# Reading the decode's gate sums from a small SBUF tile that ScalarE fills, in place of PSUM

## The chip, the core and the metric

The kernel runs on one core of a Trainium2 chip. TensorE (PE in the profile, with PEld for its weight loads) multiplies matrices into PSUM; VectorE (DVE) and ScalarE (ACT) do the elementwise work and read PSUM; GpSimd (POOL) does small elementwise work and issues gathers; SyncE (SP) issues most of the other transfers. Each engine takes its own instructions in the order in which the program lists them. The metric is the device time of one execution in microseconds (us), lower is better; the median of several executions stands for a kernel.

## What is computed

One layer of a decoder for two groups of rows that share the weights: a prompt of 1024 rows and eight sample rows, each of these with a paged cache of 8192 earlier positions. The part that the change touches is the attention of the eight sample rows. Every cached position and head carries a forget logit; a score is the query times the key plus a sum of these logits from behind that position up to the end:

```python
lf_all = jnp.concatenate([logf_pool[page_table].reshape(B, past, H).astype(jnp.float32), logf], axis=1)
c = jnp.cumsum(lf_all, axis=1)
...
s = jnp.einsum('bqhd,bkhd->bhqk', q, k).astype(jnp.float32) * (ATT_HEAD_DIM ** -0.5)
s = s + (cq.astype(jnp.float32).transpose(0, 2, 1)[:, :, :, None]
         - ck.astype(jnp.float32).transpose(0, 2, 1)[:, :, None, :])
p = jax.nn.softmax(s, axis=-1).astype(v.dtype)
return jnp.einsum('bhqk,bkhd->bqhd', p, v)
```

## The kernel before

The prompt's work (`prompt`, large matrix products with fp32 values split into a high and a low part, three products each: lines 270 to 274) and the samples' work (`sample`, which is `decode` and then `sample_rest`) are written as two Python generators. The loop at line 1923 runs the prompt's generator and, by a table of paces (`PACE`, line 76), takes pieces of the samples' generator in between. That fixes the order in which instructions are written; the order in which each engine gets them is worked out when the program is built, by a scheduler that walks a simulated timeline (`schedule_with_timeline_sim=True`, line 2013) and takes on each engine what is ready there. Some blocks bind that order: `behind(e)` (line 1369) keeps an instruction behind a named earlier one of the same engine, and `tc.high_priority()` moves one up.

`decode` (line 1374) handles the samples one after the other, sixteen chunks of keys each. For sample b, `kstep` (line 1425) has GpSimd gather a chunk of keys into a `kv` buffer (line 1428), and VectorE multiplies them with the query and sums them into the scores `s` (lines 1435 and 1436 while the prompt is in its attention, lines 1444 and 1448 elsewhere). There are four `kv` buffers, which keys and values share; `vstep` (line 1487) gathers values (line 1489), and TensorE multiplies them with the exponentials (line 1495).

In chunk 11 of a sample, `gates_scan` gathers the sample's logits (line 1404); ScalarE reorders them from position-major to head-major into the tile `A` (line 1407), and VectorE makes running sums over the 64 positions of each partition and head (line 1408). In chunk 13, `gates` (line 1411) adds the last running sum of each head to a small term (`tot`, line 1413). TensorE multiplies `tot` with a constant matrix of ones and zeros (line 1418), which gives in PSUM, in a tile `ms`, the sum over all later partitions: 128 x 8 numbers. VectorE then subtracts `A`, read with a step of 64 elements, from those 8 numbers, each broadcast over 64 positions, into the tile `dec` (line 1420). `soft_max` (line 1457) adds `dec` to the scores in line 1460, after the sixteenth chunk.

The tile `ms` has one buffer, one bank of PSUM (`MS`, line 152). It is free for its next user only when the last reader is done. The other users are the samples' softmax (lines 1468 and 1481), the later samples' stage, and the prompt's attention in its first half: there every third of the small accumulators comes from `MS` and the others from `BB` (`B3`, line 825), for the transposes of line 836 and the products of line 852. ScalarE empties these with lines 843 and 861, or VectorE with line 841.

Weights for the prompt come from memory into `wr`; ScalarE rounds them into `wh` (line 235) and VectorE subtracts to get `wl` (line 236); five and four buffers of these stand between the two engines and TensorE.

Of the kernel before, what the change touches and what calls it, by code (L numbers as in the profile page):

```python
# [11 lines left out]
AF = mybir.ActivationFunctionType  # L12
ALU = mybir.AluOpType
# [5 lines left out]
P = 128  # L19
# [59 lines left out]
def build(nc, tc, ctx, a, phases=None):  # L79
# [27 lines left out]
    def nm(s):  # L107
        cnt[0] += 1
        return f"{s}_{cnt[0]}"
# [16 lines left out]
    def sm(shape, tag, bufs=2, dt=F32):  # L126
        return small.tile(shape, dt, tag=tag, bufs=bufs, name=nm(tag))
# [24 lines left out]
    def MS():  # L152
        return BB() if MB else psum.tile([P, 512], F32, tag="ms", bufs=1, name=nm("ms"))
# [1215 lines left out]
    def behind(e):  # L1369

        return tc.issue_after(last[e]) if e in last else nullcontext()


    def decode():
# [36 lines left out]
        def gates(b, A):  # L1411
            tot = sm([P, 8], "tot", 2)
            nc.vector.tensor_tensor(
                tot, A.rearrange("p (h k) -> p h k", k=64)[:, :, 63], lfz[:, b * 8 : b * 8 + 8], op=ALU.add
            )
            ps = MS()
            with behind(ENG.PE):
                mmul(ps[:, :8], suf, tot, start=True, stop=True)
            dt_ = dec("dec").rearrange("p (k h) -> p k h", h=8)
            nc.vector.tensor_tensor(  # L1420
                dt_, ps[:, :8].unsqueeze(1).broadcast_to((P, 64, 8)), A.rearrange("p (h k) -> p k h", k=64), op=ALU.subtract
            )
            return dt_

# [99 lines left out]
        st, A, dt_, pm, dg, dv, vm = ([None] * 8 for _ in range(7))  # L1524
        pend = []
        st[0] = prep(0)
        for g in range(8 * 16 + 16 + VLAG + 2):
# [8 lines left out]
            if b < 8:  # L1536
                left = yield from kstep(b, ch, st[b])
                if ch == 11:
                    A[b] = gates_scan(b)
                if ch == 13:  # L1540
                    dt_[b] = gates(b, A[b])
                if ch == 14 and b < 7:
                    st[b + 1] = prep(b + 1)
                if ch == 15:
                    pm[b] = soft_max(b, st[b], dt_[b])
# [489 lines left out]
```

## Time and profile before

| | |
|---|---|
| runs of the kernel before (us) | 1798.83, 1797.29, 1791.11; median 1797.29 |
| the profiled execution (us) | 1793.69, of which 1791.7 lie in the profile's span |
| granted TensorE clock in it | 0.993 of full speed |
| transfers | 521.06 MB, mean 291 GB/s |

A row of the profile that begins with a line number is a group of instructions: line, engine, operation, tiles written and read, shapes, count, then busy microseconds and the mean nanoseconds of one, then the engine's idle time just before them and who ended it. A row of the instructions of one line gives, after the count, the minimum, median and maximum duration in nanoseconds and the first and the last start. A row of the timeline begins with the start and the duration in microseconds; an "x" count behind it is the number of neighbouring instructions merged. A row of waits gives the total, the number and the longest. A row of the table by stages gives the stretch, its length, and the busy time of each engine with its number of instructions, then clock, DMA share and GB/s.

### The profile page before, as it was taken

The numbers are of one execution on the slowest core, as the hardware profiler recorded it, in microseconds if no ns is written. First come the engines' busy times: TensorE is split into PE (matmuls) and PEld (weight loads), VectorE is DVE, ScalarE is ACT, GpSimd is POOL, SyncE is SP. The second block draws the span as 40 slices with busy tenths as digits, with TensorE's granted clock in tenths as the row PEclk, the third lists the DMA queues.
The fourth block names the chain that finished last, engine by engine and source line by source line (L and its number), as shares of the span: only waits on it lengthen the run. The fifth ranks groups of instructions, "written<-read, shape, count | busy, mean of one in ns | idle before, by whom it ended". The sixth has DMA issues, their size and how long they took to land.

```text
span 1791.7 us, 25124 instructions
## 1 busy us (share of the span) xinstructions
PE 1735.9 (97%) x9653; PEld 1285.7 (72%) x9653; DVE 1399.9 (78%) x1733; ACT 733.5 (41%) x1374; POOL 488.3 (27%) x461
## 2 busy tenths in 40 slices
PE   8999999889999999999999999999999999999997
PEld 5787777655677666767777777766666778768875
DVE  4689658989788986989999999898885549855344
ACT  6332355566643635333333244335353233333232
POOL 1252234443222332333322223433322112102110
PEclk9999999999999999999999999999999999999999
DMA  8786798777697975779788788988879587568982
GB/s 291 297 304 226 294 334 319 259 264 244 254 403 279 363 299 224 282 285 345 290 301 313 291 317 311 376 306 346 320 280 350 214 306 249 191 260 297 359 310 80
DMA packets 157074, 521.06 MB, mean 291 GB/s; under 512 B 20874, under 2 KB 40842, under 8 KB 124186
## 3 DMA queue, kind: packets, MB, share of 16 engines
q0 software_dynamic: 57168, 341.14, 50.0%
q1 hardware_dynamic: 92874, 165.73, 26.5%
q10 hardware_dynamic: 6912, 12.59, 1.9%
q8 instruction: 76, 1.25, 0.3%
q14 instruction: 44, 0.36, 0.1%
HBM read 495.47 MB, written 23.93 MB: 290 GB/s over the span
## 4 chain that ended last, share of the span: by engine, by line
PE 53%; issue 9%; DMA 8%; DVE 6%; ACT 2%; POOL 2%; POOLq 0%; DVEq 0%; ACTq 0%; SPq 0%
DMA kv<-cache_v,io 6%; PE ba L272 6%; PE ba L274 6%; PE ba L273 6%; PE dv L1495 4%; PE bb L272 3%; PE bb L273 3%; PE bb L274 3%; PE ba L1063 1%; DVE s L1448 1%; PE ba L1064 1%; PE ba L1065 1%; PE dv L331 1%; DMA kv<-cache_k,io 1%; PE dv L1774 1%
## 5 line engine op out<-in xcount | busy, mean ns | idle before, releaser
L235 ACT ACTIVATE wh<-wr 128x1024 fp32r<-128x1024 f32 (+2 forms) x220 | 228.6, 1044 | 443.3 <-PE ba L273 142.3
L236 DVE TENSOR_TENSOR wl<-wr,wh 128x1024 fp32r<-128x1024 f32 (+2 forms) x220 | 262.7, 1200 | 165.1 <-PE ba L274 57.4
L1428 POOL DMA_INDIRECT kv<-cache_k,io x128 | 186.9, 1460 | 606.8 <-DVE s L1448 327.2
L1444 DVE TENSOR_TENSOR kv<-kv,d 128x1024 f32<-128x1024 f32 (+1 forms) x156 | 258.0, 1681 | 32.6 <-DMA kv<-cache_k,io 32.6
L1448 DVE TENSOR_REDUCE s<-kv 128x16 f32<-128x1024 f32 (+1 forms) x156 | 258.4, 1672 | 0.0
L1489 POOL DMA_INDIRECT kv<-cache_v,io x128 | 160.8, 1256 | 239.4 <-PE dv L1495 155.2
L272 PE MATMUL ba<-u,wh 128*128 128x512 f32 x528 | 209.3, 397 | 0.0
L274 PE MATMUL ba<-u,wl 128*128 128x512 f32 x528 | 209.0, 396 | 0.0
L273 PE MATMUL ba<-u,wh 128*128 128x512 f32 x528 | 208.5, 395 | 0.5 <-DVE u L239 0.5
L272 PE MATMUL ba<-wh,u 128*128 128x512 f32 (+1 forms) x495 | 186.1, 379 | 0.9 <-ACT u L235 0.9
L273 PE MATMUL ba<-wl,u 128*128 128x512 f32 (+1 forms) x495 | 185.1, 375 | 1.3 <-DVE wl L236 1.3
L274 PE MATMUL ba<-wh,u 128*128 128x512 f32 (+1 forms) x495 | 183.4, 375 | 0.0
L1495 PE MATMUL dv<-kv,s 128*32 128x512 f32 x1024 | 127.1, 598 | 1.6 <-DMA kv<-cache_v,io 1.6
L274 PEld LDWEIGHTS ba<-u,wl 128*128 128x128 f32 x528 | 99.2, 188 | 29.0 <-issue 6.5
L272 PEld LDWEIGHTS ba<-u,wh 128*128 128x128 f32 x528 | 99.3, 188 | 26.4 <-issue 4.8
L273 PEld LDWEIGHTS ba<-u,wh 128*128 128x128 f32 x528 | 99.2, 188 | 25.2 <-issue 2.3
L272 PEld LDWEIGHTS ba<-wh,u 128*128 128x128 f32 x495 | 93.0, 188 | 25.0 <-issue 6.5
L272 PE MATMUL bb<-u,wh 128*128 128x512 f32 x272 | 108.7, 400 | 0.0
L274 PE MATMUL bb<-u,wl 128*128 128x512 f32 x272 | 108.0, 398 | 0.0
L273 PE MATMUL bb<-u,wh 128*128 128x512 f32 x272 | 107.9, 397 | 0.0
L273 PEld LDWEIGHTS ba<-wl,u 128*128 128x128 f32 x495 | 93.0, 188 | 20.1 <-DVE wl L236 1.9
L274 PEld LDWEIGHTS ba<-wh,u 128*128 128x128 f32 x495 | 92.9, 188 | 19.5 <-issue 1.6
(454 smaller groups left out, 3310.6 us busy)
## 6 DMA issues: line engine op xcount, KB each, us to landing
wr<-w_up SPq DMA_DIRECT2D x88, 512.0 KB
kv<-w_up POOLq DMA_DIRECT2D x22, 1024.0 KB
wr<-w_down SPq DMA_DIRECT2D x40, 512.0 KB
kv<-w_down POOLq DMA_DIRECT2D x11, 1024.0 KB
wr<-w_in SPq DMA_DIRECT2D x16, 512.0 KB
wr<-w_o SPq DMA_DIRECT2D x16, 512.0 KB
wr<-w_cq SPq DMA_DIRECT2D x16, 512.0 KB
wr<-w_co SPq DMA_DIRECT2D x16, 512.0 KB
```

What stands on the lines that cost most here:

```text
L235: nc.scalar.activation(h, src, AF.Copy)
L236: nc.vector.tensor_tensor(l, src, h.bitcast(F32), op=ALU.subtract)
L272: mmul(out, sh, mh, start=(i == 0), stop=False)
L273: mmul(out, sh, ml, start=False, stop=False)
L274: mmul(out, sl, mh, start=False, stop=(i == n - 1))
L331: mmul(ps[32 * j : 32 * j + 32, :w], xT[:, k, :] if nk == 8 else xT[:, k * 8 : k * 8 + 32], raw[:, q, j * w : (j + 1) * w], start=(k == 0) ...
L1063: mmul(pss[i], mh[k][:, tb], wh, start=(k == korder[0]), stop=False)
L1428: nc.gpsimd.indirect_dma_start(kv, None, a["cache_k"], off(kidx[:, b, ch : ch + 1]))
L1444: nc.vector.tensor_tensor(kvv[:, i : i + m, :], kvv[:, i : i + m, :], qb.unsqueeze(1).broadcast_to((P, m, 512)), op=ALU.mult)
L1448: nc.vector.tensor_reduce(s[:, ch * 4 + i : ch * 4 + i + m, :].rearrange("p k h -> p (k h)"), kvv[:, i : i + m, :].rearrange("p k (h d) -> ...
L1489: nc.gpsimd.indirect_dma_start(kv, None, a["cache_v"], off(kidx[:, b, ch : ch + 1]))
L1495: mmul(dv[32 * j : 32 * j + 32, :], s[:, ch * 4 : ch * 4 + 4, :].rearrange("p k h -> p (k h)"), kvv[:, j, :], start=(ch == 1), stop=(ch == ...
```

## The change

```diff
             ps = MS()
             with behind(ENG.PE):
                 mmul(ps[:, :8], suf, tot, start=True, stop=True)
+            sfs = sm([P, 8], "sfs", 2)
+            nc.scalar.activation(sfs, ps[:, :8], AF.Copy)
             dt_ = dec("dec").rearrange("p (k h) -> p k h", h=8)
             nc.vector.tensor_tensor(
-                dt_, ps[:, :8].unsqueeze(1).broadcast_to((P, 64, 8)), A.rearrange("p (h k) -> p k h", k=64), op=ALU.subtract
+                dt_, sfs.unsqueeze(1).broadcast_to((P, 64, 8)), A.rearrange("p (h k) -> p k h", k=64), op=ALU.subtract
             )
```

`sfs` is an SBUF tile of 128 x 8 fp32 numbers with two buffers. ScalarE copies the eight columns of `ms` into it; VectorE's subtraction takes the broadcast operand from `sfs`. So `ms` has ScalarE's copy as its only reader, and the subtraction waits for ScalarE where it waited for TensorE. Each of the eight samples runs this once.

## The prediction

> **What bounds the kernel now.** I read the page's busy times first, then the table by stages, then what TensorE waited for.
>
> ```profile
> span 1791.7 us, 25124 instructions
> ...
> PE 1735.9 (97%) x9653; PEld 1285.7 (72%) x9653; DVE 1399.9 (78%) x1733; ACT 733.5 (41%) x1374; POOL 488.3 (27%) x461
> ```
>
> TensorE is idle for 1791.7 - 1735.9 = 55.8 us in all. An edit that leaves TensorE's own work as it is can win some of that and no more; it can lose without such a limit. The stages show where the idle time lies (columns: stretch, its length, then the busy time of each engine):
>
> ```profile
> core 0: us, PE busy (x) PEld busy (x) DVE busy (x) ACT busy (x) POOL busy (x), PEclk, DMA share, GB/s
> ...
> 270.00:505.00 235.00, 214.97 (x1378) 152.24 (x1377) 206.36 (x356) 141.07 (x309) 82.73 (x106) 0.97 0.78 276
> ...
> 700.00:1000.00 300.00, 298.49 (x1419) 223.30 (x1418) 279.84 (x261) 105.72 (x167) 86.35 (x63) 1.00 0.78 294
> 1000.00:1150.00 150.00, 149.21 (x716) 112.03 (x716) 140.32 (x146) 57.15 (x92) 46.49 (x33) 1.00 0.87 325
> ```
>
> From 270 to 505 us, the prompt's attention, TensorE idles 235 - 214.97 = 20.0 us, more than a third of the whole, because it takes turns with VectorE and ScalarE over small tiles. From 700 to 1150 us it idles 1.5 + 0.8 = 2.3 us, though VectorE is busy for 279.84 + 140.32 = 420.2 of 450 us: there VectorE works ahead by the weight buffers. So a change on VectorE or ScalarE is worth something at once in the attention, and elsewhere only once it eats the lead.
>
> What TensorE waited for in the first half of the attention, longest first:
>
> ```profile
> PE ms L852 <- DVE dec L1420: 2.7, 1, 2.7
> PE bb L872 <- ACT t L861: 2.1, 3, 1.1
> ```
>
> The first row is the very instruction that the change edits: the products of line 852 wanted the one `ms` bank and VectorE had not yet read it. It happened once, for the second sample. This is the place, engine by engine:
>
> ```profile
> 314.39 0.34 PE L1418 MATMUL ms<-tot,cp 128*128 128x8 f32 x2
> 314.59 0.41 PE L836 MATMUL bb<-cp,t 128*128 128x128 f32 x2
> 317.72 1.55 PE L852 MATMUL ms<-t,u 128*64 128x256 f32 x8 [2.72 <-DVE dec L1420]
> ```
>
> ```profile
> 315.04 1.22 DVE L236 TENSOR_TENSOR wl<-wr,wh 128x1024 fp32r<-128x1024 f32 x1
> 316.18 0.55 DVE L813 TENSOR_REDUCE mx<-ba 128x1 f32<-128x384 f32 x1
> 316.64 1.02 DVE L1420 TENSOR_TENSOR dec<-ms,d 128x512 f32<-128x512 f32 x1
> 317.69 1.41 DVE L774 TENSOR_TENSOR u<-ba,u 64x512 fp32r<-64x512 f32 x2
> ```
>
> ```profile
> 314.37 0.58 ACT L757 ACTIVATE u<-ba 64x512 fp32r<-64x512 f32 x1
> ...
> 314.98 0.59 ACT L757 ACTIVATE u<-ba 64x512 fp32r<-64x512 f32 x1
> 315.59 0.38 ACT L843 ACTIVATE t<-bb 128x256 f32<-128x256 f32 x1
> 316.76 0.58 ACT L814 ACTIVATE t<-ba,mx 128x384 f32<-128x384 f32 x1 [0.79 <-DVE mx L813]
> ```
>
> The sums were in PSUM at 314.73, VectorE had two other instructions ahead of line 1420, and the bank came free at 316.64 + 1.02 = 317.66. TensorE stood from 315.00 on.
>
> **The change part by part.** First, VectorE's operand. Line 1420 and three rows to hold it against:
>
> ```profile
> L1420 DVE TENSOR_TENSOR dec<-ms,d x8: 1021/1063/1084, 150.4 to 1286.2; 128x512 f32<-128x512 f32 x8
> ```
>
> ```profile
> L1483 DVE TENSOR_TENSOR s<-s,ms x8: 669/678/689, 194.6 to 1332.3; 128x512 f32<-128x512 f32 x8
> ```
>
> ```profile
> L1460 DVE TENSOR_TENSOR s<-s,dec x8: 668/682/693, 173.9 to 1323.0; 128x512 f32<-128x512 f32 x8
> ```
>
> Line 1483 also broadcasts eight numbers out of `ms`, with its other operand dense, and takes 678 ns; line 1460 has both operands dense in SBUF and takes 682. PSUM as such costs nothing here. What line 1483 lacks is the step of 64 elements with which line 1420 reads `A`, and that stays. The bounds for eight of them are 0 and 8 x (1063 - 682) = 3.0 us less on VectorE; I take 0, since the row that differs by the PSUM operand alone shows no difference.
>
> [...]
>
> Second, ScalarE's eight copies. Nearest rows, a smaller and a larger copy out of `ms`:
>
> ```profile
> L1791 ACT ACTIVATE d<-ms x11: 175/197/198, 1638.8 to 1715.9; 128x32 f32<-128x32 f32 x11
> ```
>
> ```profile
> L861 ACT ACTIVATE t<-ms x10: 371/381/384, 291.1 to 465.0; 128x256 f32<-128x256 f32 x10
> ```
>
> Between 0.17 and 0.38 us each, 0.2 taken (128 x 32 is nearest): 1.6 us on an engine busy 733.5 of 1791.7 us. ScalarE's idle time hides it; without that cover it would cost the 1.6 us, 3.0 at most. No transfer is issued, moved or added.
>
> Third, the bank. In the second sample the copy can run at 314.98 if it goes ahead of the second line 757, and at the latest in the gap from 315.97 to 316.76, since line 814 there waits for VectorE's maximum. The bank is free at 315.2 or 316.2 in place of 317.66, and TensorE starts 2.5 or 1.5 us earlier. VectorE's instructions keep their times, and what follows at 317.69 (line 774) is still due to VectorE, so part may come back as a later wait. Bounds: 0 and 2.7 us gained; 1.5 taken, the later placing.
>
> Fourth, the new wait. VectorE's line 1420 now waits for ScalarE. Behind it in VectorE's queue stand the key products and the `wl` subtractions that TensorE needs. How much room there is, from the matrix product's start to the subtraction's:
>
> ```profile
> L1418 PE MATMUL ms<-tot,cp x16: 170/242/256, 149.1 to 1281.8; 128*128 128x8 f32 x16
> ```
>
> The first pair stands at 149.1 and 150.4, the last at 1281.8 and 1286.2: 1.3 and 4.4 us, of which the product takes 0.3 and a copy 0.2. I take 0. If ScalarE's head at that moment is a weight conversion that waits for TensorE, this row prices it:
>
> ```profile
> ACT wh L235 <- PE ba L273: 142.3, 54, 4.3
> ```
>
> 142.3 / 54 = 2.6 us, at most 4.3. Even eight such waits (21 us of VectorE, 34 at most) fall on stretches where VectorE has spare time (450 - 420.2 = 29.8 us from 700 to 1150 alone) and the weight buffers a lead; for TensorE I bound it by 0 and 5 us, a fourth of the 21.
>
> The sum: 0 + 0 - 1.5 + 0 = -1.5 us. The profiled execution took 1793.69, 1.99 us more than its span, and lies 3.6 us under the median of the runs shown. Against itself it goes to 1792.2; against the median, to 1795.8, say 1796. That is a tenth of a per cent. Under 0.5% (9.0 us) I call it the same, which is about what a measurement of this kernel can tell from no change.
>
> **The rivals.** *A worse order (slower).* The order on each engine is not written out; the scheduler makes it from a simulated timeline. The row of line 1413 shows how far it departs from the text:
>
> ```profile
> L1413 DVE TENSOR_TENSOR tot<-d,lfz x8: 129/156/186, 144.9 to 1230.9; 128x8 f32<-128x8 f32 x8
> ```
>
> For the last sample `tot` ran at 1230.9 and the product that stands right below it in the code at 1281.7, 51 us later. An added ScalarE instruction and a bank that is free earlier change what is ready when, from the first sample at 149 us on, and every choice behind it can fall differently. The place where that costs is 700 to 1150 us, where VectorE has 29.8 us to spare and TensorE loses 2.3: if key products are put ahead of `wl` subtractions there, TensorE begins to wait as in the attention (20.0 of 235 us, 8.5%). Half of that share over 450 us is 19 us: 1797.3 + 19 = 1816; from some 10 us of new waits on it counts as slower, 1807. For it: VectorE is busy 93% there. Against it: the written order, the priorities and `behind` are the same, and the added instruction is 0.2 us on a half-idle engine.
>
> *A better order (faster).* The same re-dealing, with the attention's waits shortened: if half of its 20.0 us goes, 1797.3 - 10 = 1787. For it: the largest single wait there is the one removed, and the chain behind it is shifted. Against it: the next waits in the list are for ScalarE, which gets more work, and 1783 would need 14 of the 20.
>
> *The bank is not freed earlier.* The scheduler may put the copy behind line 814's pair, or another user in the bank. Then nothing moves but 1.6 us on ScalarE: 1797.3, within the same class.
>
> **How the numbers follow.** The forecast with the last rival beside it, both within 0.5%: 0.39. A worse order by over 9 us: 0.35. A better one: 0.26. I give the re-dealt orders this much because nothing in the trace bounds them except TensorE's idle time on the one side. The likeliest case alone spans 1790 to 1803: the sum's bounds (-2.7 to +5) on the median and the runs' own spread. For eight in ten I go down to 1782 and up to 1818; that leaves about a twelfth below and a ninth above.
>
> **What would show it.** Right: no wait of line 852 on line 1420 at the second sample, line 1420 still near 1.06 us, a ScalarE copy near 0.2 us, and TensorE's idle time from 270 to 505 us down by 1 to 3 us. Wrong in the operand: line 1420 near 0.68 us. Wrong in the wait: ScalarE as the releaser of line 1420 with microseconds beside it. The worse order: more idle time of TensorE between 700 and 1150 us, waits for `wl` or `u`, and instructions of VectorE in another order than before. What would make the forecast wrong is that the order changes far from the eight places of the edit.

## The result, and the profile after

The changed kernel took 1810.93 us (median of 6 runs, 1807.91 to 1814.14). The kernel before, beside it, took 1794.2 (6 runs, 1787.89 to 1798.83). The ratio is 1.0095, with a 95% interval from 1.0068 to 1.0122: slower by about one per cent. (The ratios in this document are estimated from all runs on both sides and are not the quotients of the medians; the two differ by up to 0.2 per cent.) The profiled execution took 1809.02 us, of which the span is 1807.3.

The page of the changed kernel, first its span and then the busy times:

```profile
span 1807.3 us, 25152 instructions
...
PE 1742.2 (96%) x9653; PEld 1289.6 (71%) x9653; DVE 1399.9 (77%) x1733; ACT 732.8 (41%) x1382; POOL 498.2 (28%) x461
```

The span grew by 15.6 us, TensorE's busy time by 6.3, so its idle time by 9.3. VectorE has the same 1399.9 us of work as before; the change gave it nothing to do and took nothing away. TensorE's matmuls are the same 9653, so the 6.3 us are matmuls that ran more slowly or overlapped less. GpSimd gained 9.9 us, though its work is the same. Two things to explain, then: what GpSimd's extra time is, and why TensorE both waits longer and runs slower.

At its own eight places the edit did what the prediction said. Two groups, the subtraction and the copy of the changed kernel (count, then minimum/median/maximum in ns):

```profile
L1422 DVE TENSOR_TENSOR dec<-sfs,d x8: 1065/1078/1089, 149.9 to 1295.6; 128x512 f32<-128x512 f32 x8
```

```profile
L1420 ACT ACTIVATE sfs<-ms x8: 158/178/178, 147.9 to 1292.4; 128x8 f32<-128x8 f32 x8
```

The subtraction is at 1078 ns where it was at 1063, and a copy takes 0.18 us. (Lines behind the edit are two higher than before: 1422 is the old 1420, 1430 the old 1428, 1491 the old 1489.) The second sample's place in the timeline of the changed kernel:

```profile
318.62 0.34 PE L1418 MATMUL ms<-tot,cp 128*128 128x8 f32 x2
...
319.21 0.59 ACT L757 ACTIVATE u<-ba 64x512 fp32r<-64x512 f32 x1
...
319.83 0.18 ACT L1420 ACTIVATE sfs<-ms 128x8 f32<-128x8 f32 x1
...
320.06 1.14 PE L852 MATMUL ms<-t,u 128*64 128x256 f32 x8 [0.82 <-ACT sfs L1420]
...
321.70 1.06 DVE L1422 TENSOR_TENSOR dec<-sfs,d 128x512 f32<-128x512 f32 x1
```

TensorE's wait there fell from 2.72 to 0.82 us, because the bank comes free at 320.01 and not at the end of the subtraction, which is now put off to 321.70. That is 1.9 us gained on the spot. It doesn't reach the end. Some 15 us later a wait for ScalarE comes that is as long as the one removed; line 836 had waited for line 814 for 0.4 us in all in the first half of the attention before.

```profile
335.89 0.75 PE L836 MATMUL bb<-cp,t 128*128 128x128 f32 x3 [2.72 <-ACT t L814]
```

Over the whole attention TensorE is idle for 235 - 213.36 = 21.6 us, where it was idle for 20.0 before and the prediction wanted 1 to 3 us less:

```profile
270.00:505.00 235.00, 213.36 (x1385) 150.84 (x1384) 202.35 (x353) 142.41 (x317) 80.97 (x105) 0.99 0.79 275
```

Where the time went is read by setting the n-th matmul of TensorE against the n-th of before, for each kernel from its span's start; both kernels have 9653 matmuls. The difference in start time (us, worked out from the traces; the rows e1 to e10 are the experiments described below, and in e8 and e9 the program is that of before, with something added behind its end):

```
matmul number          800  1000  1600  2000  2800  3600  4000  6000  6400  6800  7600  9600
before, at (us)        149   194   313   389   518   677   762  1183  1267  1346  1495  1770
after                 -1.5  +4.4  +4.2  +2.9  +3.6  +7.8  +8.5  +8.1 +10.3 +14.0 +14.4 +15.3
e1_first_only         -1.9  +2.8  +2.8  +0.4  +0.2  +0.8  +0.8  +2.6  +3.3  +1.1  +1.1  +1.1
e2_rest_only          -1.7  -1.4  -1.5  -2.9  -4.1  +2.3  +3.2  +2.8  +5.4  +9.0  +9.4 +10.2
e3_second_only        -1.5  -1.5  -1.5  -4.5  -4.0  +2.4  +2.1  +3.3  +5.7  +9.8 +10.2 +11.2
e4_copy_psum_read     -1.3  -1.3  -1.5  -2.7  -2.5  -1.8  -1.8  -2.1  -2.0  -4.2  -4.2  -3.9
e5_other_bank         -1.3  -1.3  -1.4  -4.4  -3.3  +1.5  +1.5  +0.9  +3.1  +6.6  +7.0  +8.9
e6_copy_in_bank       -1.0  -1.0  -1.1  -1.9  -2.1  +2.6  +3.2  +2.2  +7.3  +5.1  +5.1  +5.2
e7_vector_copy_second -1.9  -1.6  -1.8  -3.9  -4.0  -3.9  -3.8  -2.2  +1.0  -0.1  -0.1  -0.1
e8_probe              -0.3  -0.3  -0.1  -1.6  -1.7  +2.3  +2.2  +1.5  +1.1  -1.1  -1.1  -1.1
e9_probe_independent  -0.8  -0.8  -0.9  -2.4  -2.2  -2.2  -2.2  -2.5  +1.8  -0.4  -0.3  -1.1
e10_all_but_second    -1.1  +5.0  +4.9  +2.5  +2.4  +6.4  +6.4  +8.1  +8.1  +6.0  +6.0  +6.0
```

In the changed kernel +5.9 us come in one step at the first sample's gates (between 149 and 194 us of before), 4.2 between 518 and 677, 2.2 between 1183 and 1267, and 3.7 between 1267 and 1346. From 762 to 1183 us nothing is lost.

The rows e8 and e9 show how much single executions of one program differ: by up to 4.5 us at 677 us. So a difference of some 4 us in one row says little, and what counts is what recurs. Between 1183 and 1346 us the changed kernel and the three experiments with its order (e2, e3, e5) all lose 5.7 to 6.5 us, and the other seven rows lie between -2.6 and +2.9. Between 518 and 677 us those four lose 4.2 to 6.4 us, but three of the others (e6, e8, e10) lose 4.0 to 4.7 there too.

**The first step, at 149 us.** The timeline of the kernel before, GpSimd and then VectorE:

```profile
149.76 1.21 POOL L1428 DMA_INDIRECT kv<-cache_k,io  x1 [1.25 <-DVE cc L537]
```

```profile
149.48 0.67 DVE L236 TENSOR_TENSOR t<-t,t 8x512 fp32r<-8x512 f32 x1
150.08 0.41 DVE L545 TENSOR_SCALAR t<-t 8x512 f32<-8x512 f32 x1
150.41 1.07 DVE L1420 TENSOR_TENSOR dec<-ms,d 128x512 f32<-128x512 f32 x1
```

And of the changed kernel, where the order of every engine is still the same:

```profile
149.23 9.51 POOL L1430 DMA_INDIRECT kv<-cache_k,io  x1 [1.24 <-DVE cc L537]
```

```profile
149.55 0.41 DVE L545 TENSOR_SCALAR t<-t 8x512 f32<-8x512 f32 x1
149.89 1.09 DVE L1422 TENSOR_TENSOR dec<-sfs,d 128x512 f32<-128x512 f32 x1
150.90 0.41 DVE L545 TENSOR_SCALAR t<-t 8x512 f32<-8x512 f32 x1
151.24 6.68 DVE L1446 TENSOR_TENSOR kv<-kv,d 128x2048 f32<-128x2048 f32 x3
157.84 2.27 DVE L1450 TENSOR_REDUCE s<-kv 128x32 f32<-128x2048 f32 x1
```

GpSimd's issue of one gather of keys takes 9.51 us in place of 1.21. Before, it ended at 150.97, 0.56 us into the subtraction with the PSUM operand. After, it ends at 158.74, 0.9 us into the reduction at 157.84, the first long operation that reads a single tile. In between VectorE does nothing but operations with two SBUF inputs and two short multiplications by a constant (0.41 us). What came of it, in VectorE's and TensorE's timelines of the changed kernel and in its table by stages (granted clock, DMA share and GB/s end the row):

```profile
163.40 2.29 DVE L1446 TENSOR_TENSOR kv<-kv,d 128x2048 f32<-128x2048 f32 x1 [3.29 <-DMA kv<-cache_k,io]
```

```profile
166.88 0.80 PE L273 MATMUL ba<-wl,u 128*128 128x512 f32 x1 [3.24 <-DVE wl L236]
167.48 0.63 PE L274 MATMUL ba<-wh,u 128*128 128x512 f32 x1
...
172.90 0.39 PE L273 MATMUL ba<-wl,u 128*128 128x512 f32 x1
```

```profile
163.00:167.00 4.00, 0.76 (x3) 0.30 (x2) 3.60 (x3) 0.00 (x0) 0.00 (x0) 0.80 0.78 290
167.00:171.00 4.00, 4.00 (x10) 3.13 (x11) 4.00 (x3) 0.52 (x1) 1.69 (x1) 0.50 0.49 145
171.00:175.00 4.00, 4.00 (x17) 3.20 (x16) 4.00 (x4) 0.54 (x1) 2.38 (x1) 0.84 0.89 313
```

The keys of the late gather held up VectorE for 3.29 us, its `wl` came late, and TensorE waited 3.24 us. During this wait the granted clock fell to 0.50, where it stayed for 6.83 us, from 165.4 to 172.3, and the next matmuls took 0.63 us each. The wait put TensorE 3.4 us back (from -1.52 to +1.88, matmul by matmul); the slow clock cost 2.5 more (to +4.39).

**The later steps.** From the second sample's gates on the instructions stand in another order: in the traces some 1190 of TensorE's 9653 matmuls stand at another place than before, the first of them behind that gate, and so do 285 of VectorE's 1733 instructions and 24 of GpSimd's 461. One place of the new order, first GpSimd's row of before, then the changed kernel's timeline, GpSimd, VectorE and TensorE:

```profile
568.17 0.94 POOL L1489 DMA_INDIRECT kv<-cache_v,io  x1 [0.30 <-PE bb L274]
```

```profile
572.11 6.68 POOL L1491 DMA_INDIRECT kv<-cache_v,io  x1 [0.30 <-PE bb L274]
```

```profile
572.16 2.34 DVE L1446 TENSOR_TENSOR kv<-kv,d 128x1024 f32<-128x1024 f32 x2
574.42 1.21 DVE L236 TENSOR_TENSOR wl<-wr,wh 128x1024 fp32r<-128x1024 f32 x1
575.56 0.14 DVE L1474 TENSOR_TENSOR mT<-m,snT 8x1 f32<-8x1 f32 x1
575.63 2.34 DVE L236 TENSOR_TENSOR wl<-wr,wh 128x1024 fp32r<-128x1024 f32 x2
577.90 2.33 DVE L1450 TENSOR_REDUCE s<-kv 128x16 f32<-128x1024 f32 x2
```

```profile
587.28 1.92 PE L1497 MATMUL dv<-kv,s 128*32 128x512 f32 x16 [2.74 <-DMA kv<-cache_v,io]
```

Here six operations with two SBUF inputs stand in a row, GpSimd's issue of a gather of values lasts until 0.9 us into the reduction behind them, and TensorE waits 2.74 us for the values of this very gather. Before, the issue of the same gather took 0.94 us, and the longest wait for values in that stretch was 0.3 us. And near the end of the samples, two waits of the changed kernel (total, times, longest), and the stage behind them:

```profile
PE ba L280 <- ACT u L238: 1.3, 2, 1.2
PE ba L1124 <- DVE u L239: 1.2, 1, 1.2
```

```profile
1340.00:1350.00 10.00, 9.23 (x51) 8.70 (x52) 6.79 (x16) 5.37 (x15) 0.56 (x1) 0.68 0.25 102
```

The granted clock is 0.68 on the average of these 10 us; it is 0.50 for 6.83 of them and 1.00 for the rest. Before, it was 1.00 throughout this part:

```profile
1340.00:1350.00 10.00, 10.00 (x56) 6.93 (x55) 6.42 (x8) 5.49 (x8) 1.93 (x2) 1.00 0.56 185
```

In e2, e3 and e5 the clock is 0.72, 0.77 and 0.66 from 1330 to 1340 us. In all kernels without this order it is 1.00 there and from 1340 to 1350.

### The profile page after: what moved, and what is told of

Its sections match the earlier page's. It is cut to its first block, busy times and chain, and to the rows that moved or that the text cites. A ratio compares the mean times of both kernels' runs of the same rounds, so it can differ in the third digit from the quotient of the medians.

```text
span 1807.3 us, 25152 instructions
## 1 busy us (share of the span) xinstructions
PE 1742.2 (96%) x9653; PEld 1289.6 (71%) x9653; DVE 1399.9 (77%) x1733; ACT 732.8 (41%) x1382; POOL 498.2 (28%) x461
## 4 chain that ended last, share of the span: by engine, by line
PE 43%; issue 11%; DMA 9%; DVE 6%; POOL 3%; ACT 2%; POOLq 0%; DVEq 0%
DMA kv<-cache_v,io 6%; PE ba L272 5%; PE ba L274 5%; PE ba L273 5%; PE dv L1497 4%; PE bb L274 3%; PE bb L272 3%; PE bb L273 3%; DMA kv<-cache_k,io 2%; DVE kv L1446 1%; PE dv L331 1%; PE ba L1064 1%; PE ba L1065 1%; PE dv L1776 1%; PE ba L1063 1%
## 5 line engine op out<-in xcount | busy, mean ns | idle before, releaser
L1430 POOL DMA_INDIRECT kv<-cache_k,io x128 | 190.7, 1490 | 589.2 <-DVE s L1450 325.0
L1491 POOL DMA_INDIRECT kv<-cache_v,io x128 | 168.7, 1318 | 270.1 <-PE dv L1497 200.2
```

Of the source, the lines that this page charges most:

```text
L1430: nc.gpsimd.indirect_dma_start(kv, None, a["cache_k"], off(kidx[:, b, ch : ch + 1]))
L1491: nc.gpsimd.indirect_dma_start(kv, None, a["cache_v"], off(kidx[:, b, ch : ch + 1]))
```

## The experiments

Each kernel is the one before with the edit shown. "Order" below is the order of the instructions on each engine.

**e1: the copy in the first sample alone.** The order is exactly that of before.

```diff
+            sums = ps[:, :8]
+            if b == 0:
+                sums = sm([P, 8], "sfs", 2)
+                nc.scalar.activation(sums, ps[:, :8], AF.Copy)
-                dt_, ps[:, :8].unsqueeze(1)...
+                dt_, sums.unsqueeze(1)...
```

> The edit for the first sample alone; the other seven read PSUM as before. Every engine's order is that of the kernel before, with one ScalarE copy more. Theory A (GpSimd's issue of the key gather at 149 us is held up while VectorE runs instructions with both inputs in SBUF; the subtraction's PSUM operand had let it through): that issue takes 9 to 10 us in place of 1.2, TensorE loses some 6 us between 150 and 175 us and the time is 5 to 7 us (0.3 to 0.4%) over before. Theory B (all of the loss is the scheduler's new order, which starts at the second sample): the same as before within 2 us. Theory C (VectorE's wait for ScalarE's copy costs): under 1 us.

Measured: 1795.97 us against 1795.02, ratio 1.0013 (0.9994 to 1.0032). The long issue is there:

```profile
148.54 9.51 POOL L1432 DMA_INDIRECT kv<-cache_k,io  x1 [1.25 <-DVE cc L537]
```

That the SBUF operand makes it, and not the copy or the wait for ScalarE, is shown by e4 and e6 below: they have these with the operand in PSUM, and there the issue takes 1.21 us. Its step in the table is 4.7 us (-1.9 to +2.8), of which 2.4 are won back in the attention (+2.8 to +0.4); the rows e8 and e9, which had lost nothing, go down by 1.5 there as well. What is left in the measured time, 1.0013, is too small to tell from nothing, where theory A had 0.3 to 0.4%.

**e2: the copy in all samples but the first** (`if b > 0` in the same edit; the order is that of the changed kernel).

> The edit for samples two to eight; the first reads PSUM as before. Every engine's order is that of the changed kernel less one ScalarE copy. Theory A with a new order as the second cause: the issue at 149 us takes about 1.2 us, the step of 6 us between 150 and 175 us is gone, and the time is 9 to 11 us over before, 6 under the changed kernel. Theory B: all 15 us over before. Theory C: seven eighths of the 15.

Measured: 1806.4 against 1795.02, 1.0073 (1.0051 to 1.0095). The first gates' issue is back at 1.21 us and the step at 149 us is gone; the later ones are all there.

```profile
149.29 1.21 POOL L1432 DMA_INDIRECT kv<-cache_k,io  x1 [1.25 <-DVE cc L537]
```

**e3: the copy in the second sample alone** (`if b == 1`; TensorE, GpSimd and SyncE have the order of the changed kernel).

> The edit for the second sample alone. The order on TensorE, GpSimd and SyncE is that of the changed kernel (a few rows differ on ScalarE and VectorE late in the program). If the second sample's earlier release of the bank starts the new order and that order costs the rest: 9 to 11 us over before, as the run with the edit for samples two to eight. If the later samples' edits cost something of their own by the same hold-up of gathers: less than that run by 2 us or more.

Measured: 1805.6 against 1795.02, 1.0075 (1.0049 to 1.0102). One copy of eight gives most of the loss, and with the same long issue:

```profile
564.45 6.68 POOL L1493 DMA_INDIRECT kv<-cache_v,io  x1 [0.30 <-PE bb L274]
```

**e4: the copies without their use.** ScalarE copies in all eight samples, VectorE reads PSUM as before. The order is nearly that of before (in the traces 9 of TensorE's matmuls, 3 of ScalarE's instructions and 11 of VectorE's stand elsewhere).

```diff
+            sfs = sm([P, 8], "sfs", 2)
+            nc.scalar.activation(sfs, ps[:, :8], AF.Copy)
```

> ScalarE copies the sums for all eight samples, but VectorE's subtraction still reads PSUM; the copy's result is not used. Order nearly that of the kernel before. Theory A: no long issue at 149 us, the time of before within 3 us. If the ScalarE copies themselves or the second reader of the bank cost: over before by more than 3 us.

Measured: 1792.8 against 1795.02, 0.9996 (0.9982 to 1.0011). ScalarE's eight copies cost nothing that shows.

**e5: the second sample's sums in another bank, with no copy at all.** VectorE reads PSUM everywhere; the `ms` bank is free for the prompt because the second sample doesn't take it. All but three places of TensorE's order are the changed kernel's; GpSimd's and SyncE's are the same.

```diff
-            ps = MS()
+            ps = BB() if b == 1 else MS()
```

> The kernel before, but the second sample's sums go to a buffer of the other small PSUM pool (bb) in place of ms. No ScalarE copy, no SBUF operand, no wait for ScalarE; ms is simply not occupied by that sample. The order this gives on TensorE, GpSimd and SyncE is, but for 3 places of TensorE, that of the changed kernel. If the new order by itself costs: 0.6 to 0.9% over before, as the run with the edit for the second sample alone (0.75%), with the long issue of a value gather near 564 us and the loss near 1320 to 1340 us in the trace. If the SBUF operand or the wait for ScalarE costs: the same as before within 0.2%.

Measured: 1806.44 against 1798.01, 1.0046 (1.0029 to 1.0063), less than expected but slower, with the same place in its timeline:

```profile
565.13 6.67 POOL L1489 DMA_INDIRECT kv<-cache_v,io  x1 [0.31 <-PE bb L274]
```

So neither the copy, nor the SBUF operand, nor a wait for ScalarE is needed for the larger part of the second sample's loss. What the three kernels e2, e3 and e5 share is that the prompt's bank isn't held at the second sample, and with it the new order. Why this kernel loses 0.46% and the one with the second copy 0.75%, with nearly the same order, stays open; the intervals overlap.

**e6: the hop with the bank held.** ScalarE copies the sums to eight other columns of the same bank and VectorE reads them there: the wait for ScalarE without the early release and without the SBUF operand, in all samples.

```diff
+            sums = ps[:, 8:16]
+            nc.scalar.activation(sums, ps[:, :8], AF.Copy)
-                dt_, ps[:, :8].unsqueeze(1)...
+                dt_, sums.unsqueeze(1)...
```

> ScalarE copies the sums for all eight samples into eight other columns of the same ms tile, and VectorE reads them there. So the wait for ScalarE is that of the changed kernel, the operand is in PSUM and the bank is held until VectorE is done. Order nearly that of the kernel before (7 places of TensorE and 11 of VectorE differ). If order and operand are the causes: within 0.3% of before and no issue of 9 us at 149 us. If VectorE's wait for ScalarE costs: over 0.5%.

Measured: 1797.78 against 1798.01, 1.0004 (0.9986 to 1.0022). The new wait costs nothing that shows, as the prediction's fourth term had it, and the first gate's issue takes 1.21 us.

**e7: an early release by VectorE.** In the second sample VectorE copies the eight columns, ahead of what it has queued, and subtracts from the copy. That frees the bank early too, but gives a third order.

```diff
+            if b == 1:
+                sums = sm([P, 8], "sfs", 2)
+                with tc.high_priority():
+                    nc.vector.tensor_copy(sums, ps[:, :8])
```

> For the second sample alone VectorE itself copies the sums to SBUF at high priority and then subtracts. The bank is free early, and the scheduler makes a third order, other than both kernels'. If a new order is a draw that can fall either way: anywhere from -0.5% to +0.9%. If an early release of the bank is bad in itself: +0.6% or more, as the two runs that release it early in another way.

Measured: 1794.41 against 1798.01, 0.9979 (0.9966 to 0.9992). This is the only version that came out ahead of before, and it frees the bank early as well, at 314.87 + 0.16 = 315.03 us; TensorE's wait falls from 2.72 to 1.23 us:

```profile
314.87 0.16 DVE L1423 COPY sfs<-ms 128x8 f32<-128x8 f32 x1
```

```profile
315.08 1.84 PE L852 MATMUL ms<-t,u 128*64 128x256 f32 x8 [1.23 <-DVE sfs L1423]
```

Its order departs from that of before in fewer than 400 of the 9653 matmuls. So the early release isn't bad in itself, and what is left to decide is the order that follows from it. No run keeps before's order with the bank released early, so the order's part is shown by this contrast and not by itself.

**e8: the long issue by itself, first try.** Behind the finished kernel GpSimd issues a gather while VectorE runs ten operations of 128 x 512 of one kind, each kind twice. (This and the next probe only add work and time behind the kernel.)

```
nc.vector.tensor_tensor(t, kv[:, :512], w, op=ALU.mult)      # lets the gather start
nc.gpsimd.indirect_dma_start(kv, None, a["cache_k"], ...)
for _ in range(10):
    nc.vector.tensor_tensor(t, t, w or ps, op=ALU.mult)      # or a reduction of t, or t times a constant
```

> The kernel before with a probe behind its end: ten times an indirect gather from the key cache, issued by GpSimd while VectorE runs ten instructions of 128 x 512 in a row, of four kinds: multiply with both inputs in SBUF, multiply with one input in PSUM, reduce with one input, multiply by a constant; each kind twice. If VectorE with two SBUF inputs holds up GpSimd's issue: 6 to 7 us of issue in that kind and 0.9 to 1.3 us in the PSUM and the reduce kind; the constant kind is open. If only the schedule around 149 us was at work: 0.9 to 1.3 us in all.

Measured, the issues under two SBUF inputs, a PSUM operand, a reduction and a constant:

```profile
1804.97 1.27 POOL L1960 DMA_INDIRECT kv<-cache_k,probe  x1 [5.54 <-DVE u L1959]
1812.96 0.94 POOL L1960 DMA_INDIRECT kv<-cache_k,probe  x1 [6.72 <-DVE u L1959]
1820.97 0.94 POOL L1960 DMA_INDIRECT kv<-cache_k,probe  x1 [7.07 <-DVE u L1959]
1828.91 1.00 POOL L1960 DMA_INDIRECT kv<-cache_k,probe  x1 [7.00 <-DVE u L1959]
```

A miss: two SBUF inputs cost 0.33 us more and not the whole run; the second round of the four kinds gave the same durations. But these ten operations are a chain on one tile, so that each waits for the one before it (10 in 7.23 us, a start every 0.72 us against a duration of 0.69). In the kernel neighbours overlap.

**e9: second try, with operations that don't depend on each other**: all read the same two tiles and each writes its own; a mixed kind has one PSUM operand among ten.

```
for k in range(10):
    nc.vector.tensor_tensor(outs[k], t, ps if kind == "psum" or (kind == "mixed" and k == 4) else w, op=ALU.mult)
```

> The last probe's ten operations formed a chain on one tile, with some 30 ns between neighbours. Here ten operations that do not depend on each other (all read the same two tiles or the same bank, each writes its own 128 x 512 tile) follow each issue of a GpSimd gather, behind the finished kernel, each kind twice; in a fifth kind, the mixed one, the fifth of ten operations with two SBUF inputs reads PSUM in place of one of them. Theory: neighbours that overlap leave GpSimd no opening while each has two SBUF inputs. Then the issue lasts until the run's end (about 6 to 7 us in all) under the SBUF kind, about 3 us (to the fifth operation) under the mixed kind, and 0.9 to 1.3 us under the PSUM operand, the reduction and the multiply by a constant. Rival: a run of two-SBUF-input operations as such does not hold the issue, and what held it in the kernel is in the tile that GpSimd or VectorE works on or in the transfers; then all five kinds stay at 0.9 to 1.3 us as in the chained probe. Only these rows are read from it; the probe comes on top of the whole kernel, so its total time is some 60 to 90 us above before.

Measured, two SBUF inputs, mixed, PSUM, reduction, constant:

```profile
1803.70 1.27 POOL L1964 DMA_INDIRECT kv<-cache_k,probe  x1 [5.56 <-DVE u L1963]
1810.57 1.27 POOL L1964 DMA_INDIRECT kv<-cache_k,probe  x1 [5.60 <-DVE u L1963]
1817.44 0.94 POOL L1964 DMA_INDIRECT kv<-cache_k,probe  x1 [5.60 <-DVE u L1963]
1824.27 0.94 POOL L1964 DMA_INDIRECT kv<-cache_k,probe  x1 [5.89 <-DVE u L1963]
1831.05 1.00 POOL L1964 DMA_INDIRECT kv<-cache_k,probe  x1 [5.84 <-DVE u L1963]
```

A miss again, in both rounds, though the ten now overlap (6.11 us for ten). "A run of such operations holds the issue" is too strong. So I counted in the traces of ten kernels (before, after, e1 to e7 and e10) every gather issue that began while VectorE had over 0.08 us left of an operation with two SBUF inputs, and asked whether it was done within 1.1 us of that operation's end:

```
what VectorE did next                                          done    held on
an idle gap first                                               157          0
overlapping, one input or an operand in PSUM                    429          3
overlapping, again two SBUF inputs                              253        204
```

Behind an overlapping neighbour with two SBUF inputs the issue is held on in 204 of 457 cases, 45%; behind anything else in 3 of 589. The probes drew few times, each kind at one and the same phase, and got in. (Most of these places recur in all ten traces, so the cases are not independent of each other.) What decides between the 253 and the 204 isn't settled, but the phase has a part in it: of the issues that began within 0.6 us of the running operation's start 194 were held on and 153 were not, of those that began later 10 and 100.

The three exceptions are the first gate's own issue, in the changed kernel, e1 and e10. The operation next in line there is the multiplication by a constant of 0.41 us (line 545), the same in all ten kernels. With a PSUM operand behind it the issue came through in all seven kernels that have one, with an SBUF operand in none of the three. So that short operation with a single input is not an opening by itself at this place, though runs of such multiplications let the issue in in the probes (1.00 us); and at the first gate the outcome never varied.

**e10: seven of the eight samples changed, the second not** (`if b != 1`). The order is before's on TensorE, GpSimd and SyncE.

> The change as it was made for seven of the eight samples; only the second (b == 1) keeps the PSUM operand and its bank. The order on TensorE, GpSimd and SyncE is then before's, and VectorE's and ScalarE's differ in 9 and 3 places. Theory: the loss is the order that is dealt again when the second sample's bank comes free early, plus the first gate's longer gather issue. Then this kernel stands where the kernel with the first copy alone stood: ratio 1.000 to 1.003, with the 9 us issue near 149 us and no value gather of 6.7 us near 564 us. Rival: the copies and the SBUF operand cost something in every sample; then seven eighths of the loss are here, 1.007 to 1.009.

Measured: 1801.27 against 1796.81, 1.0028 (1.0011 to 1.0045). In its trace the loss is the step at 149 us, of which the attention again gives part back (+5.0 to +2.5), and 4.0 us between 518 and 677. With the latter goes one issue in this kernel's timeline, against the same issue of before:

```profile
606.53 5.08 POOL L1432 DMA_INDIRECT kv<-cache_k,io  x1 [1.67 <-DVE s L1452]
```

```profile
603.32 1.67 POOL L1428 DMA_INDIRECT kv<-cache_k,io  x1 [0.54 <-DVE s L1448]
```

The order is the same there and no gate is near, so a shift of the phase was enough. The program of before did the same in one execution, the one with the probe e8 behind its end, and lost 4.0 us in this stretch against the profiled before:

```profile
602.17 5.09 POOL L1428 DMA_INDIRECT kv<-cache_k,io  x1 [1.66 <-DVE s L1448]
```

The hop with the bank held, with PSUM operands everywhere, had this same issue at 5.08 us in its trace (602.08), and 4.7 us more in the same stretch, though its median equals before's. So a single profiled execution holds such draws of some 4 us that the median of many doesn't; the 9.5 us at the first gate came in all three traces with an SBUF operand there, and the 6.7 us near 564 us (572 in the changed kernel) in all four traces of the new order.

## Why the prediction was wrong

**The terms of the edit held.** VectorE's own duration didn't change (1063 to 1078 ns, term 0). ScalarE's copies took 0.18 us each (0.2) and cost nothing that shows, by the kernel that copies without using it. The wait of line 852 fell by 1.9 us where 1.5 were taken. The new wait cost nothing that shows, by the hop in the bank. These four together are the sum of -1.5 us, and on the spot nothing speaks against it; that it would be left over in the attention's idle time did not come true (21.6 us against 20.0). One reading was looser than it said: lines 1483 and 1460 differ by the broadcast as well as by the PSUM operand, which did no harm here.

**What failed is the step that let the rest stand still.** The third part says "VectorE's instructions keep their times, and what follows at 317.69 (line 774) is still due to VectorE". In the changed program they don't follow in that order: with the bank free at the second sample, the scheduler chose otherwise there, line 1422 came behind the first line 774, and some 1190 of TensorE's matmuls moved. This was the rival "a worse order", which had 1816 us and a chance of 0.35; 1810.93 is that case and not the forecast. The range of 1782 to 1818 holds it thanks to this rival and not to the sum. One copy in the second sample gives 1.0075 of the 1.0095, and freeing the bank with no copy gives 1.0046. So my reason against it, "the added instruction is 0.2 us on a half-idle engine", weighed the wrong thing. It isn't the size of the added instruction that deals the order again, but the earlier moment at which a resource comes free, and that moment was the very term that I counted as the gain. (With the copies and no early release, in e4 and e6, the order hardly changed.)

**The rival had the mechanism but not the place.** It named 700 to 1150 us and "from the first sample at 149 us on". The order is unchanged up to the second sample, and from 762 to 1183 us the changed kernel loses nothing (+8.5 to +8.1). Hardly anything moved there: from 640 to 1185 us TensorE, GpSimd and SyncE have the order of before, and only nine places of VectorE and three of ScalarE near 860 us differ. So whether VectorE's 29.8 us to spare would have been eaten was not tried. The losses lie from 518 to 677 us, with a late gather, and from 1183 to 1346, where the rows of waits name ScalarE's copies (lines 1175, 1209, 238) and VectorE's subtractions (236, 239). In the attention TensorE's wait fell in the `ms` row (2.72 to 0.82) and rose for line 814 (0.4 to 3.7).

**The operand has a second price that I left at zero.** "I take 0, since the row that differs by the PSUM operand alone shows no difference" is right for VectorE's time and says nothing of GpSimd's. In the traces, at the first gate the two-input operation with an operand in PSUM was an opening through which GpSimd's gather issue came, and in SBUF it isn't: 1.21 against 9.51 us, in the same order, in all three kernels with an SBUF operand there (after, e1, e10) and in none of the seven with PSUM. The row of before already showed it: the issue of 149.76 ended 0.56 us into line 1420. The counts over ten traces point the same way: behind an overlapping neighbour with two SBUF inputs the issue was held on in 204 of 457 cases, behind anything else in 3 of 589. By what path VectorE holds GpSimd up, no run shows. For the total time this price is small: 1.0013 alone, with an interval that holds 1, and 1.0028 for seven samples, of whose trace 4.0 us came at 606 us by phase.

**The parts add up.** 0.28% (seven samples without the second) and 0.75% (the second alone) make 1.03%, and the whole change measured 0.95% (0.68 to 1.22).

**The price of a wait was too low.** The prediction took a wait for its length. A wait of 3.24 us cost 5.9, because the clock fell to 0.50: 2.5 us on top at 167 us and, by half of 6.83, up to 3.4 at 1340 us. Over the whole span the clock went only from 0.993 to 0.991, since other stretches of the new order ran at a higher one than before (0.99 against 0.97 from 270 to 505 us).

**The better order** had 0.26 and exists: the early release by VectorE's own copy came out at 0.9979. From the profile of before I see no way to have told which of the orders the scheduler would deal.

## What to carry to other kernels

In a program whose order a scheduler makes, an edit that frees a resource earlier isn't priced by the wait that it removes: it deals the order again from that point on, which here was worth between -0.2% and +0.75%, more than the wait. Hold the order against the old one before believing a local gain, and try the release in more than one form. Moving an operand out of PSUM can also close an opening for GpSimd's gathers when its neighbours on VectorE have two SBUF inputs (at the first gate here the issue took 9.51 us in place of 1.21), so look at the durations of the gather issues near it.

## What the runs showed of the hardware that I had not expected

An issue of a gather by GpSimd, 0.93 us at best in the kernel before, took up to 9.51 us while VectorE ran overlapping operations with two SBUF inputs, and whether it got in at a boundary between two of them varied with the phase (253 to 204). An idle gap, or an operation with a PSUM operand or a single input, let it in in 586 of 589 cases; the other three are the first gate's, where a single-input operation of 0.41 us did not.

In the twelve traces TensorE's granted clock went with how busy a whole window of 3.41 us had been, and not with the length of one wait alone. It is 1.00 or 0.50 in all of them, and within a trace it changes only at whole multiples of 3.41 us from its other changes. TensorE's busy share in each such window at full clock, set against the clock of the next one, gives:

```
busy share of the window      windows    next window at 0.50
under 0.41                         38                     38
0.41 to 0.61                       88                     22
over 0.61                        6069                      0
```

What decides among the 88 windows in the middle isn't shown. The wait of 3.24 us, in a window busy for 0.48, brought 6.83 us at 0.50 and cost 5.9 us in place of 3.4; the wait of 2.74 us at 587 us left a window at 0.41 and brought none. At 1336 us several waits, none above 1.2 us, together left a window at 0.39, and 6.83 us at 0.50 followed.
